# A gated linear unit on one core: the odd tiles' stores issued by GpSimd instead of the scalar engine

## The chip, the cores and the metric

The kernel runs on one core of one Trainium2 chip. The metric is the device time of one execution in microseconds (us); a smaller number is better. The time before is 932.57 us, the median of three runs.

## The reference

```python
x: float32 [8192, 8192]
a, b = np.split(x, 2, axis=-1)
return a * (1 / (1 + np.exp(-b)))      # float32 [8192, 4096]
```

Each output row is the left half of an input row, multiplied element by element by the sigmoid of the right half. So 268 MB are read and 134 MB written.

## The kernel before

A tile is 256 rows of x: 128 partitions with two neighbouring rows each, so that a partition's share of a tile is one contiguous run of 64 KB on the way in and of 32 KB on the way out. There are 32 tiles. Two input buffers `xs` (x_sb in the profile, 64 KB of each partition) and two output buffers `os` (o_sb, 32 KB) are used in turn: tile i uses buffer i % 2 of both, so even tiles have one pair of buffers and odd tiles the other.

`load(i)` (line 63) is a DMA on SyncE's queue, one for a whole tile (two halves for tile 0). `store(i, ...)` (line 68) is a DMA on the scalar engine's queue, one for a whole tile; tile 0 has two pieces of 2 MB, tile 31 one of 2 MB and two of 1 MB. In the profile q1 is SyncE's queue and q10 the scalar engine's.

`work(i, ...)` computes a tile. For tiles 1 to 30 a no-operation on TensorE (line 87) first joins two waits: the tile's load has landed, and the store of tile i-2, which leaves the same output buffer, has landed. Then ScalarE takes the sigmoid of the whole right half in place (line 92). The product (line 97) is split by columns: GpSimd multiplies the first 3/16 (for tile 1 VectorE does), then VectorE the rest; VectorE's instruction waits for GpSimd's. Tiles 0 and 31 are computed in fourths by ScalarE and VectorE alone, so that their stores can start early.

The main loop is: work on tile i, then `load(i + 2)`, then the store of tile i. Both wait for VectorE's product. The order in which each engine gets its instructions is the order of this loop; it is not rearranged (`place` keeps program order and drops the waits that follow from others). On GpSimd's instruction stream there are only the products of tiles 2 to 30, some set-up at the start, and the closing waits and semaphore clears that `_close_on_sync` puts at the end. There SyncE waits for the last store alone; GpSimd waits for the other queues' semaphores and clears them.

Of the kernel before, what the change touches and what calls it, by code (L numbers as in the profile page):

```python
# [8 lines left out]
def _tiles(ctx, tc, x, out):  # L9
    nc = tc.nc  # L10
# [8 lines left out]
    SLOTS = 2  # L19
    n_tiles = n_rows // (P * R)  # L20
    x_g = x.rearrange("(g p h r) m -> g h p (r m)", p=P, h=2, r=R)
    out_g = out.rearrange("(g p h r) m -> g h p (r m)", p=P, h=2, r=R)
# [3 lines left out]
    os = [pool.tile([P, R * half], fp32, name=f"o_sb{k}") for k in range(SLOTS)]  # L26
# [15 lines left out]
    def meet(a, b):  # L42
        return a[0] < b[1] and b[0] < a[1]
# [4 lines left out]
    def place(i, ins, *needs):  # L48


        kept = {n.ins.name for n in needs}
        for e in traced[i % SLOTS]:
            if e.ins.name not in kept:
                tc.declare_no_dep(ins.ins, e.ins, reason="follows from the waits that are kept")
        traced[i % SLOTS].append(ins)
        tc.keep_in_program_order(ins)
        return ins
# [7 lines left out]

    def store(i, lo, hi):
        c = slice(lo * half // 4, hi * half // 4)
        ins = nc.scalar.dma_start(out=out_g[i // 2, i % 2, :, c], in_=os[i % SLOTS][:, c])  # L68
        done = [m for w, m in mul_of[i] if meet(w, (lo, hi))]
        store_of.setdefault(i, []).append(((lo, hi), place(i, ins, *done)))  # L70

# [32 lines left out]
    for i in range(n_tiles):  # L104
        due = list(stores[i])
        for k, piece in enumerate(works[i]):
            work(i, *piece)
            ready = works[i][k - behind[i]][1] if k >= behind[i] else 0
            while len(stores[i]) > 1 and k < len(works[i]) - 1 and due[0][1] <= ready:
                store(i, *due.pop(0))  # L110
        if i + SLOTS < n_tiles:
            load(i + SLOTS)
        for lo, hi in due:
            store(i, lo, hi)
# [115 lines left out]
```

## Time and profile before

| what | value |
|---|---|
| median of 3 runs (lowest to highest) | 932.57 us (932.52 to 932.69) |
| the profiled execution's own time | 932.44 us |
| its span in the profile | 931.1 us |
| busy: VectorE, ScalarE, GpSimd | 232.5, 227.0, 99.3 us |
| moved by DMA | 402.67 MB, mean 432 GB/s |
| issue to landing, median: a whole load, a whole store | 40.0 us, 40.2 us |

The page gives busy times of the compute engines, the share of time in which the core's 16 DMA engines were busy, and the bytes of each DMA queue. The chain of waits names, going back from the last instruction, what released each step. A DMA's "landing" is the time from its issue until its semaphore says that all of it has arrived, so it includes the time spent queued behind other transfers.

### The profile page before, as it was taken

How to read it: one execution, taken by the hardware profiler on the slowest of the kernel's cores; microseconds unless marked ns; L12 is line 12 of the kernel's file. 1: busy time of each engine (PE TensorE's matmuls, PEld its weight loads, DVE VectorE, ACT ScalarE, POOL GpSimd, SP SyncE). 2: the span in 40 equal slices, each digit the busy share in tenths (PEclk: the TensorE clock that was granted, in tenths of full speed). 3: DMA queues.
4: the chain of work that ended last, by engine and by line, in shares of the span. 5: the costliest groups of instructions: out<-in, count | busy, mean ns of one | idle time of the engine just before them, and what ended most of it. 6: DMA issues, size and time to landing. Idle time of an engine off the chain costs nothing.

```text
span 931.1 us, 299 instructions
## 1 busy us (share of the span) xinstructions
DVE 232.5 (25%) x39; ACT 227.0 (24%) x39; POOL 99.3 (11%) x33
## 2 busy tenths in 40 slices
DVE  1133203332023320233302333023330233311333
ACT  2123332033320333202332023320233202333023
POOL 0001110111101111011110111101111011110110
DMA  9999999999999999999999999999999999999998
GB/s 405 450 442 414 428 450 425 453 405 428 450 428 450 410 469 405 428 450 428 450 405 459 420 428 451 425 450 408 431 448 428 450 408 467 408 428 450 427 452 383
DMA packets 9793, 402.67 MB, mean 432 GB/s; under 512 B 1088, under 2 KB 1088, under 8 KB 1088
## 3 DMA queue, kind: packets, MB, share of 16 engines
q1 hardware_dynamic: 4752, 268.44, 66.6%
q10 hardware_dynamic: 5040, 134.22, 33.4%
q14 instruction: 1, 0.01, 0.0%
HBM read 268.44 MB, written 134.22 MB: 432 GB/s over the span
## 4 chain that ended last, share of the span: by engine, by line
DMA 69%; DVE 12%; ACT 12%; POOL 5%; issue 0%; PEldq 0%; ACTq 0%; SPq 0%
DMA out_dram<-o_sb 60%; DVE o_sb L97 12%; ACT x_sb L92 12%; DMA x_sb<-in_x_dram 9%; POOL o_sb L97 5%; PEldq L87 0%; ACTq L68 0%; SPq L63 0%
## 5 line engine op out<-in xcount | busy, mean ns | idle before, releaser
L97 DVE TENSOR_TENSOR o_sb<-x_sb 128x6656 f32<-128x6656 f32 (+2 forms) x39 | 232.5, 5969 | 690.3 <-POOL o_sb L97 632.7
L92 ACT ACTIVATE x_sb<-x_sb 128x8192 f32<-128x8192 f32 (+1 forms) x38 | 225.7, 5949 | 692.7 <-PEq L87 632.9
L97 POOL TENSOR_TENSOR o_sb<-x_sb 128x1536 f32<-128x1536 f32 x29 | 99.1, 3417 | 793.9 <-ACT x_sb L92 793.9
L92 ACT ACT_TABLE_LOAD x1 | 1.3, 1283 | 0.8 <-PEq L214 0.8
L214 POOL MEMSET const-float32-0.0<- 128x1 f32 x1 | 0.1, 99 | 0.2 <-issue 0.2
L214 POOL MEMSET const-bfloat16-1.0<- 128x1 bf16 x1 | 0.1, 103 | 0.0
L214 POOL MEMSET const-uint8-127<- 128x1 uint8 x1 | 0.1, 103 | 0.0
L214 POOL MEMSET const-float32-1.0<- 128x1 f32 x1 | 0.1, 99 | 0.0
## 6 DMA issues: line engine op xcount, KB each, us to landing
out_dram<-o_sb ACTq DMA_DIRECT2D x30, 4096.0 KB, 40.2
x_sb<-in_x_dram SPq DMA_DIRECT2D x2, 4096.0 KB, 16.6
out_dram<-o_sb ACTq DMA_DIRECT2D x3, 2048.0 KB, 27.8
out_dram<-o_sb ACTq DMA_DIRECT2D x2, 1024.0 KB, 8.3
x_sb<-in_x_dram SPq DMA_DIRECT2D x31, 40.0
```

What stands on the lines that cost most here:

```text
L92: before = nc.scalar.activation(out=g, in_=g, func=SIG)
L97: mul = engine.tensor_mul(out=packed[:, r, c], in0=rows[:, r, 0, c], in1=b)
L214: nc = _bacc.Bacc("TRN2", target_bir_lowering=False, num_devices=1)
```

## The change

The store of a tile with an odd number, except the last tile (31), is issued by GpSimd on GpSimd's own DMA queue. The stores of the even tiles and of tile 31 stay on the scalar engine's queue. Those are 15 whole-tile stores, of tiles 1, 3, ..., 29. What is waited for, the buffers, the loads and the arithmetic stay as they are.

```diff
     def store(i, lo, hi):
         c = slice(lo * half // 4, hi * half // 4)
-        ins = nc.scalar.dma_start(out=out_g[i // 2, i % 2, :, c], in_=os[i % SLOTS][:, c])
+        odd = i % 2 and i < n_tiles - 1
+        ins = (nc.gpsimd if odd else nc.scalar).dma_start(out=out_g[i // 2, i % 2, :, c], in_=os[i % SLOTS][:, c])
         done = [m for w, m in mul_of[i] if meet(w, (lo, hi))]
         store_of.setdefault(i, []).append(((lo, hi), place(i, ins, *done)))
```

## The prediction

> **What bounds the kernel now.** I read the page's table of slices and queues first, then one stretch of 58 us in the middle, then the chain of waits, then the end in order of time. The page and the stretch 99.5 to 157.5 (its columns are length, busy VectorE, ScalarE, GpSimd, granted clock, DMA share, GB/s):
>
> ```profile
> DMA  9999999999999999999999999999999999999998
> q1 hardware_dynamic: 4752, 268.44, 66.6%
> q10 hardware_dynamic: 5040, 134.22, 33.4%
> 99.50:157.50 58.00, 14.18 (x2) 14.06 (x2) 6.83 (x2) 1.00 1.00 434
> ```
>
> The DMA engines are busy the whole time, at 434 GB/s. A tile moves 8.39 MB in and 4.19 MB out, 12.58 MB; 12.58 MB / 434 GB/s = 29.0 us, and two tiles make the 58.0 us of the stretch. All 402.67 MB at 434 GB/s are 928 us, so of the 931.1 us of span only some 3 us are not transfer. The change moves no byte less: a gain beyond those 3 us does not exist. The chain of waits for one pair of tiles:
>
> ```profile
> 117.35 40.23 DMA out_dram<-o_sb
> 157.58 0.03 issue
> 157.61 0.06 PEldq L87
> 157.67 0.02 issue
> 157.69 7.04 ACT x_sb L92
> 164.73 0.07 issue
> 164.80 3.43 POOL o_sb L97
> 168.23 0.02 issue
> 168.25 7.10 DVE o_sb L97
> 175.35 0.02 issue
> 175.37 40.19 DMA out_dram<-o_sb
> ```
>
> A buffer's round trip is 40.2 us of store and load in flight and 17.8 us of compute, 58.0 together: exactly two tiles' worth of transfer. The transfers set the 58, and the 40.2 is partly queueing: 29.0 us are service and 40.2 - 29.0 = 11.2 us are spent behind the previous tile's transfer in the same queue. That 11.2 us is the kernel's reserve.
>
> How the two queues share the engines matters here. The counts on the page are 33 loads x 144 packets and 35 stores x 144: 128 of data and 16 small semaphore writes each. A whole load's packet is 64 KB, a whole store's 32 KB; the trace's packet records show 2.418 and 1.213 us for them. Each of the 16 engines has 8 of each per tile. Load and store are issued together and land together (40.0 and 40.2), so the queues alternate one packet each: 8 x (2.418 + 1.213) = 29.0 us.
>
> The end, in order of time (start, length, what):
>
> ```profile
> 871.60 0.36 ACTq L68 DMA_DIRECT2D out_dram<-o_sb  x1
> ...
> 900.61 0.34 ACTq L68 DMA_DIRECT2D out_dram<-o_sb  x1
> 911.66 5.51 ACT L92 ACTIVATE x_sb<-x_sb 128x2048 f32<-128x2048 f32 x3 [21.70 <-DMA x_sb<-in_x_dram]
> ...
> 918.13 0.34 ACTq L68 DMA_DIRECT2D out_dram<-o_sb  x1
> ```
>
> Load 31 lands at 911.3; store 30 (issued 900.61) is what the engines do while tile 31's first half is computed. By the packet records it ends at 920.4 to 921.0 on the sixteen engines. The first piece of store 31 is issued at 918.13, and a DMA on an idle queue moves its first packet 1.0 us after issue (the first load's records), so it is ready at 919.1. The end is covered with 920.4 - 919.1 = 1.3 us to spare.
>
> **Part by part.** (1) ScalarE loses 15 issues of 0.36 us each. They stand in its idle time (22 us before each sigmoid): worth 0.
>
> (2) GpSimd gains 15 issues. Each store waits for VectorE's product of the same tile, as load i+2 does. Queued behind it on GpSimd is its product of tile i+1: store 3 would be issued at 117.35 and that product starts at 136.18 in the timeline, 18.8 us later. What the issue costs GpSimd is not in this trace; the nearest rows are ScalarE's 0.36 us and, as a far end, GpSimd's whole product of 3.42 us. Both vanish in 18.8 us: 0. SyncE's loads have a stream of their own, and TensorE's joining wait only names another semaphore: 0.
>
> (3) The store enters its queue later than from ScalarE, by an amount no row shows. Low end 0; far end one GpSimd instruction, 3.4 us. I take some 1 us, nearer to the 1.0 us of a DMA on an idle queue. It is covered by the 11.2 us that the store no longer spends queued. The Trainium skill (DMA: Bandwidth & Descriptors, Specifications) has about 1 us to the first byte for GpSimd's software-made descriptors and 0.6 us for the others; by these figures the term would be 0.4 us later and still covered. No run here shows it.
>
> (4) The sharing changes. An odd store no longer waits 11.2 us for the even one; for a while three queues take turns, and a turn is 2.418 + 2 x 1.213 = 4.84 instead of 3.63 us, so the load advances more slowly. No work is added: the load lands later by the store packets that overtook it, between one (1.2 us) and the three that fit in the reserve (11.2 / 3.63). Then the store lands earlier (about 30 us after issue, its bare service), the load after some 40 us, and no more packets can overtake. In the middle this costs nothing while the load queue is never empty: a load alone lasts 8 x 2.418 = 19.3 us, and beside a store 29.0, while a landed load needs 17.8 us of compute, and about 1 us to enter, before the next is queued.
>
> (5) The end is where it shows. Store 30 still ends when all transfers before it are done, but load 31 lands one to three packets later, 1.2 to 3.6 us; less the 1.3 us to spare, the engines stand idle for 0 to 2.3 us before store 31. Stepping the turns through the 32 tiles, with two packets taken ahead in each engine (store 0 is issued at 18.57 and first moves at 23.56, 1.0 us of start and about two packets), the load is one or two packets late. I take two: 2.4 - 1.3 = +1.1 us.
>
> (6) GpSimd's closing waits get the new queue's semaphore, done since about 905: 0, up to 0.5 us if its clears fall behind (the closing rows on GpSimd are 17 to 78 ns each and end 1.7 us before the span).
>
> Sum: +1.1 us on the profiled execution, 932.44 + 1.1 = 933.5; the median is 0.13 above that execution, so 933.7. From both ends of (5) and (6) the case spans 0 to +2.8: 932.5 to 935.4. What a measurement can tell from no change is 0.2%, 1.9 us, so to 934.4: this case is mostly "same".
>
> **Rivals.**
>
> *GpSimd's queue takes several packets in a turn.* Then an odd store runs through its 8 packets, 9.7 us, while load and even store stand, and the load that follows runs alone for part of its time. The queue of loads can then run dry: from a load's last byte to the issue of the next are 19.5 us here (881.1 in the packet records to 900.61), and 1 us to enter makes 20.5, against 19.3 us of a load alone. That is up to 1.2 us per pair of tiles, 15 times: 0 to +18 us, in the middle some +6, 939. For it: nothing in this trace forbids it, since GpSimd issues no DMA. Against it: both queues that are seen take one packet a turn. The Trainium skill (DMA: Bandwidth & Descriptors, Queues, rings and completion order) says that an engine drains a whole packet of typically 9 to 17 descriptors before it switches; for the two queues here the rows differ, the turn is a single 64 or 32 KB piece.
>
> *The odd store gets too small a share, or enters too late; this is the slow end.* Place: TensorE's joining wait for tiles 3, 5, ..., 31. It decides as soon as store i lands later than load i+2, about 40 us after issue. Were GpSimd's packets 16 KB, the store would need 16 turns of 2.418 + 0.61, 48.4 us, and 8 packets of the even store fall into them, 9.7: 58 us, 18 later than the load, 15 times: +275, some 1207 us. Were it whole packets but over some 6 us late, stepping the turns gives 5 to 6 us a pair, +80, 1013 us. For it: the reserve is 11 us and each late pair makes the next later. Against: a contiguous run of 32 KB is one packet on the queue seen, and no row of this core's issue is longer than 0.43 us.
>
> *Each packet of the new queue costs a little more on the engines*, 120 per engine: 0.02 to 0.1 us each is +2 to +12 us. The semaphore and data packets of the two queues show no such difference between them.
>
> *Nothing changes at all* (load 31 only one packet late): 932.5, part of my range. *Faster:* a store that starts at once could fill gaps, but all idle time is some 3 us, 1.4 of it the first packet's start and the last semaphore; a gain over 1.9 us has next to no room.
>
> **How the numbers follow.** My case (with "nothing changes" in it) 0.45; several packets a turn 0.22; dearer packets 0.13; too small a share or too late 0.17; faster 0.03. Slower by over 0.2%: 0.07 of my case (two or three packets late), 0.20 and 0.12 of the next two, 0.17: 0.56. Faster 0.03. Same: the rest, 0.41. The likeliest single case gives 933.7, its own range is 932.5 to 935.4; the range must reach over the next two rivals to leave no more than 0.2 out: to 952, the +18 with my term added. Below, 932.0.
>
> **What would show it.** Right: three queues on the page, the new one with 15 x 144 packets and 62.9 MB; DMA share 1.00 in stretches of 58 us; stores landing in about 30 us and loads still in 40; load 31 landing 1 to 4 us later, and a gap of 0 to 2 us before store 31. Several packets a turn: stores of GpSimd landing in 10 to 20 us and loads in the middle preceded by idle engines. Too late or too small a share: GpSimd's stores landing after 45 us or more, ScalarE's sigmoids of odd tiles released by a store, DMA share well under 1. Dearer packets: the stretch of 58 us longer at a share of 1.00. A time under 930.7 would make the whole account wrong.

## The result and the profile after

The changed kernel takes 935.66 us (median of 5 runs, 935.45 to 936.97) against 932.69 us before (5 runs, 932.52 to 932.75): a ratio of 1.0035, 95% interval 1.0024 to 1.0046, some 3 us slower. The profiled execution took 935.52 us, its span is 934.2 us, 3.1 us longer than before.

The middle of the kernel is as fast as before. From the page, the DMA slices, the queues, and the groups of DMA issues (their last column is the median time from issue to landing):

```profile
DMA  9999999999999999999999999999999999999998
q1 hardware_dynamic: 4752, 268.44, 66.4%
q10 hardware_dynamic: 2880, 71.30, 17.7%
q0 software_dynamic: 2160, 62.92, 15.6%
out_dram<-o_sb POOLq DMA_DIRECT2D x15, 4096.0 KB, 34.2
out_dram<-o_sb ACTq DMA_DIRECT2D x15, 4096.0 KB, 32.8
x_sb<-in_x_dram SPq DMA_DIRECT2D x31, 40.3
```

and the same stretch of 58 us as before:

```profile
99.50:157.50 58.00, 14.18 (x2) 14.06 (x2) 7.42 (x3) 1.00 1.00 434
```

There are three queues now; q0 is GpSimd's, with 15 x 144 packets. The stretch still moves 434 GB/s at a share of 1.00. But stores, of both queues, land 33 to 34 us after issue instead of 40.2, and loads still take 40. The chain of waits shows the same turn of roles: one of its round trips is

```profile
142.87 7.10 DVE o_sb L98
149.99 40.21 DMA x_sb<-in_x_dram
190.27 7.04 ACT x_sb L93
```

where before the 40 us were a store. The load has become what lands last. The end in order of time:

```profile
876.65 0.59 POOL L69 DMA_DIRECT2D out_dram<-o_sb  x1 [7.42 <-DVE o_sb L98]
...
904.18 0.34 ACTq L69 DMA_DIRECT2D out_dram<-o_sb  x1
915.46 5.51 ACT L93 ACTIVATE x_sb<-x_sb 128x2048 f32<-128x2048 f32 x3 [21.93 <-DMA x_sb<-in_x_dram]
...
921.93 0.34 ACTq L69 DMA_DIRECT2D out_dram<-o_sb  x1
```

Tile 31's first sigmoid starts at 915.46 instead of 911.66, 3.8 us later, and its first store is issued at 921.93 instead of 918.13, the same 3.8 us. The busy times around 921 us (columns as before: length, VectorE, ScalarE, GpSimd, clock, DMA share, GB/s; a DMA packet is counted here in the stretch in which it starts) show what that does:

```profile
920.50:922.50 2.00, 2.00 (x2) 0.66 (x2) 0.00 (x0) 1.00 0.08 33
```

Between 920.5 and 922.5 packets for only 33 GB/s start. In the kernel before the same two microseconds read

```profile
920.50:922.50 2.00, 2.00 (x1) 0.00 (x0) 0.00 (x0) 1.00 1.03 442
```

So the larger part of the loss is a hole at the end: store 30 is finished and store 31 isn't ready. By the packet records fourteen of the sixteen engines end store 30 at 920.8 to 921.4 and two at 922.1 and 922.3; all of them begin store 31 at 922.8 to 922.9. In the mean of the sixteen the hole is 1.7 us of the 3.1. Another 0.65 us is not a hole: the packets of the whole run took that much longer per engine (931.42 us before, 932.07 now), nearly all of it in loads of the first 100 us.

### The profile page after: what moved, and what is told of

The parts are those of the page before. It is cut to its first block, busy times and chain, and to the rows that moved or that the text cites. A ratio compares the mean times of both kernels' runs of the same rounds, so it can differ in the third digit from the quotient of the medians.

```text
span 934.2 us, 296 instructions
## 1 busy us (share of the span) xinstructions
DVE 232.5 (25%) x39; ACT 227.0 (24%) x39; POOL 108.2 (12%) x48
## 4 chain that ended last, share of the span: by engine, by line
DMA 67%; DVE 12%; ACT 11%; POOL 5%; issue 3%; PEldq 0%; ACTq 0%; POOLq 0%
DMA x_sb<-in_x_dram 63%; DVE o_sb L98 12%; ACT x_sb L93 11%; POOL o_sb L98 5%; DMA out_dram<-o_sb 5%; PEldq L88 0%; ACTq L69 0%; POOLq L69 0%
## 5 line engine op out<-in xcount | busy, mean ns | idle before, releaser
L69 POOL DMA_DIRECT2D out_dram<-o_sb x15 | 9.0, 603 | 166.1 <-DVE o_sb L98 166.1
```

What stands on the lines that cost most here:

```text
L69: ins = (nc.gpsimd if odd else nc.scalar).dma_start(out=out_g[i // 2, i % 2, :, c], in_=os[i % SLOTS][:, c])
```

## The experiments

Two theories stood against each other. *Overtaking:* a store that enters a queue of its own gets ahead of load packets, the loads are late from then on, and the only place that pays is the end. *A price for GpSimd's queue:* each store that GpSimd issues costs something (3 us / 15 = 0.2 us each), or its packets are dearer. The diffs are against the changed kernel, except where the kernel before is named.

**One store instead of fifteen.**

```diff
-        odd = i % 2 and i < n_tiles - 1
+        odd = i == 3
```

> Only the store of tile 3 is issued by GpSimd, the other 14 odd stores go back to the scalar queue. Overtaking theory: one store that enters without queueing moves the loads behind it 3 to 4 us later, and nothing later in the kernel brings them back, because the next stores then find their queue empty; load 31 lands 3 to 4 us later than before and the whole loss of about 3 us is there with one store in fifteen: 935 to 936 us. Rival, a price for each store that GpSimd issues (3 us over 15 stores, 0.2 us each): 932.9 us, and load 31 lands as before.

Measured: 935.99 us, ratio 1.0038 (1.0025 to 1.0050). One store costs as much as fifteen; a price for each is ruled out. The sigmoids of tiles 3 to 7 and then of tile 31, in order of time:

```profile
99.77 7.03 ACT L93 ACTIVATE x_sb<-x_sb 128x8192 f32<-128x8192 f32 x1 [21.98 <-PEq L88]
133.14 7.03 ACT L93 ACTIVATE x_sb<-x_sb 128x8192 f32<-128x8192 f32 x1 [26.34 <-PEq L88]
164.07 7.03 ACT L93 ACTIVATE x_sb<-x_sb 128x8192 f32<-128x8192 f32 x1 [23.90 <-PEq L88]
191.88 7.03 ACT L93 ACTIVATE x_sb<-x_sb 128x8192 f32<-128x8192 f32 x1 [20.78 <-PEq L88]
220.87 7.03 ACT L93 ACTIVATE x_sb<-x_sb 128x8192 f32<-128x8192 f32 x1 [21.96 <-PEq L88]
...
916.84 5.51 ACT L93 ACTIVATE x_sb<-x_sb 128x2048 f32<-128x2048 f32 x3 [21.93 <-DMA x_sb<-in_x_dram]
```

Before, these starts are 99.67, 129.07, 157.69, 186.68, 215.67 and 911.66. The differences are 0.1, 4.1, 6.4, 5.2, 5.2 and, 24 tiles later, 5.2 us. Store 3 enters at about 118 us, the loads behind it are set back, by 6.4 us at most, 1.2 us more than what stays, and remain 5.2 us late (3 to 4 were expected) to the end of the kernel, with nothing on GpSimd's queue any more.

**The same store on a hardware queue.** The kernel before, with store 3 on SyncE's queue ahead of load 5:

```diff
-        ins = nc.scalar.dma_start(out=out_g...
+        ins = (nc.sync if i == 3 else nc.scalar).dma_start(out=out_g...
...
+        if i == 3:
+            store(i, *due.pop())
         if i + SLOTS < n_tiles:
             load(i + SLOTS)
```

> The kernel before, with the store of tile 3 alone put on SyncE's queue, just ahead of load 5; GpSimd issues no DMA. Overtaking theory: a single store that gets ahead of a load shifts the loads for the rest of the kernel, whichever engine issues it; load 31 lands 1 to 5 us later than before and the time rises by 1 to 3.5 us, 933.7 to 936 us. Rival, the loss belongs to GpSimd's software queue: 932.6 us, as before.

Measured: 934.66 us, ratio 1.0022 (1.0013 to 1.0031). Tile 31's sigmoid starts 2.9 us late:

```profile
914.54 5.51 ACT L92 ACTIVATE x_sb<-x_sb 128x2048 f32<-128x2048 f32 x3 [21.85 <-DMA x_sb<-in_x_dram]
```

GpSimd issues no DMA here, and the loads are late all the same: the lateness belongs to the order of packets, not to GpSimd. How it costs time differs. There is no hole at the end of this run, because store 30 ends late as well (921.6 to 922.5 on the sixteen engines, 920.4 to 921.0 before). Its packets took 1.6 us longer per engine, and that is nearly all of the 1.8 us by which the span grew.

**All stores on GpSimd,** first from tile 1:

```diff
+        odd = 0 < i < n_tiles - 1
```

> All stores of tiles 1 to 30 are issued by GpSimd, so that the middle of the kernel has two queues again. Overtaking theory: store i+1 stands behind store i in one queue, as before; only at tile 1 and at the change of queue before tile 31 can a store overtake; 932.5 to 933.7 us, load 31 as before within one store packet (1.2 us). Rival, a price for each store that GpSimd issues: 30 stores, twice the loss, some 939 us.

Measured: 933.90 us, ratio 1.0021 (1.0012 to 1.0030); the runs fall into two groups, 933.5 to 933.9 (6 runs) and 935.1 to 936.6 (5 runs). That is just above the expected range and not the 939 us of a price per store, but load 31 was not within one packet as expected: in the profiled execution, one of the slower group (935.46 us), tile 31's sigmoid starts at 916.36, 4.7 us late. Tile 0's stores were still on the scalar queue, so store 1 overtook tile 0's second piece. The run is confounded by the very effect, and was repeated without the change of queue:

```diff
+        odd = i < n_tiles - 1
```

> All stores of tiles 0 to 30 are issued by GpSimd, so that no store changes its queue until tile 31 and none can overtake in the middle. Overtaking theory: loads land when they did before, within 1 us, and the time is 932.4 to 933.4 us, although GpSimd issues 32 stores. Rival, GpSimd's queue costs something of its own (each store issued some 0.3 us later and 0.6 us of issue, or dearer packets): 934 us or more, with 31 tiles instead of 15 paying.

Measured: 932.87 us, ratio 1.0002 (0.9994 to 1.0011). The groups of issues on its page, and the start of tile 31 in order of time:

```profile
out_dram<-o_sb POOLq DMA_DIRECT2D x30, 4096.0 KB, 40.0
x_sb<-in_x_dram SPq DMA_DIRECT2D x31, 40.1
```

```profile
912.15 5.51 ACT L93 ACTIVATE x_sb<-x_sb 128x2048 f32<-128x2048 f32 x3 [21.74 <-DMA x_sb<-in_x_dram]
```

With 32 stores on GpSimd and one queue for all of them until tile 31, stores land after 40.0 us again and the time is that of before. GpSimd's queue costs this kernel nothing that can be measured.

**Only the last odd store,** tile 29's (`odd = i == 29`):

> Only the store of tile 29, the last odd one before the end, is issued by GpSimd. Overtaking theory: it overtakes what is left of store 28 beside load 30 and load 31, load 31 lands 1 to 5 us later and most of the loss is there: 934 to 936 us. Rival, a price for each store: 932.8 us. A third reading, that the shift has to build up over many tiles: 932.6 to 933 us, with load 31 as before.

Measured: 938.61 us, ratio 1.0064 (1.0051 to 1.0076). More than the expected 936, and nearly twice the loss of the full change. So the shift does not have to build up. With store 3 alone it was largest just after the overtaking (6.4 us at the second sigmoid, 5.2 once settled); that the end comes here before it has settled fits this, and is not shown further. The chain of waits:

```profile
871.93 47.29 DMA x_sb<-in_x_dram
919.22 0.02 issue
919.25 1.92 ACT x_sb L93
```

Load 31 takes 47.3 us instead of 40.0; tile 31 starts 7.6 us late. A load's 144 packets are 128 of data and 16 semaphore writes, one from each engine, and it has landed when the last of these has arrived. Fifteen of load 31's were there by 916.2; the last came 3.1 us later.

Six kernels and the kernel before, one profiled execution each, all in us. "Packets" is how much longer one engine's packets took in all than before, "hole" how much longer the engines were idle between 919 and 929 us (both from the packet records, as the mean of the sixteen engines). "Spread" is the time between the first and the last of load 31's sixteen semaphore arrivals.

| kernel | tile 31 starts | later | span | longer | packets | hole | spread |
|---|---|---|---|---|---|---|---|
| before | 911.66 | | 931.1 | | | | 0.6 |
| all of tiles 0 to 30 on GpSimd | 912.15 | 0.5 | 931.6 | 0.5 | 0.1 | 0.0 | 1.0 |
| store 3 on SyncE | 914.54 | 2.9 | 932.9 | 1.8 | 1.6 | 0.05 | 1.05 |
| the change | 915.46 | 3.8 | 934.2 | 3.1 | 0.65 | 1.7 | 1.5 |
| all of tiles 1 to 30 on GpSimd | 916.36 | 4.7 | 934.1 | 3.0 | 0.7 | 2.55 | 3.7 |
| only store 3 on GpSimd | 916.84 | 5.2 | 934.6 | 3.5 | 2.3 | 1.6 | 2.9 |
| only store 29 on GpSimd | 919.25 | 7.6 | 937.0 | 5.9 | 2.3 | 3.9 | 4.1 |

Except for the first, a span is longer by the lateness of tile 31 less 0.7 to 1.7 us, around the 1.3 us to spare that the prediction read from the trace of before. But the same loss can be made up differently: in the change the hole is the larger part, with store 3 alone the longer packets. What is left of a row lies at the start and after 929 us. And where a store has overtaken, the sixteen engines no longer finish a load together. The first of load 31's arrivals is 2.9 us later than before in the change and also with store 3 alone; the last, for which tile 31 waits, is 3.8 and 5.2 us later.

**Covering the end.** The changed kernel with load 31 in two halves, so that half of tile 31 is there early:

```diff
-    loads[0] = stores[0] = rows
+    loads[0] = stores[0] = loads[-1] = rows
```

> The changed kernel, with load 31 issued as two DMAs of half a tile each, as load 0 is. Overtaking theory with the loss at the end: the first half of tile 31 is there before the whole load would be, its first store piece is ready before store 30 ends, the engines do not fall idle at the end and 1.5 to 3 us come back: 932.5 to 934.2 us. Rival, a loss spread over the middle (a price for each store, slower packets): the end has little to give, 935 us or more.

Measured: 934.01 us (11 runs), ratio 1.0015 (1.0006 to 1.0024): within the expected range. The first piece of store 31 was still issued only at 919.96, behind a sigmoid that waited for the second half. Even so, by the packet records store 31 begins at 920.8 to 921.4, as store 30 ends: the hole is gone with the halves alone. With that order mended as well:

```diff
-            ready = works[i][k - behind[i]][1] if k >= behind[i] else 0
+            late = behind[i] if k > 1 else 0
+            ready = works[i][k - late][1]
```

> The changed kernel with load 31 in two halves, and with the first piece of tile 31's store issued directly after the product it needs (in the run with halves alone it stood in ScalarE's stream behind a sigmoid that waited for the second half, and was issued only at 919.96). Overtaking theory with the loss at the end: first piece ready well before store 30 ends, idle engines at the end gone; what is left is the 0.6 us of longer packets: 932.6 to 933.6 us. Rival, loss in the middle: 934 us or more, as with halves alone.

Measured: 934.22 us, ratio 1.0016 (1.0007 to 1.0025). The first piece is issued at 911.92, and the hole is closed here too, as the busy times show:

```profile
920.50:922.50 2.00, 0.52 (x1) 2.00 (x2) 0.00 (x0) 1.00 0.90 385
```

but the time is 0.6 us above what was expected (the runs range from 933.0 to 936.7), and no better than with halves alone. By the packet records of this execution 15 of the 16 engines write their last semaphore at 930.7 to 931.2, about where the kernel before ends, and one at 933.0. So the hole's share came back on fifteen engines, and one straggler, some 2 us behind, now sets the time of this execution. The lag is not new at the end: already at 104.5 us a load's last semaphore arrives 2.1 us after the fifteenth, and the second half of load 31 is 4.2 us late in the same way (920.0 against 915.8). The run with halves alone has the same straggler (932.9, the other fifteen by 931.1). Why one engine falls behind stays open. The same two changes on the kernel before:

> The kernel before with the same two edits at the end (load 31 in halves, first piece of its store issued directly after its product). Both theories: the kernel before has under half a microsecond of idle engines at its end, so there is next to nothing to gain: 932.0 to 932.8 us.

Measured: 932.72 us, ratio 1.0008 (0.9999 to 1.0018). No gain; no version tried here beats the kernel before.

**The slow rival.** Three runs asked how far the changed kernel is from the collapse that the prediction priced. Odd stores of GpSimd in two DMAs of half the columns, 16 KB packets:

```diff
+        if i % 2 and i < n_tiles - 1:
+            due = rows
         for lo, hi in due:
             store(i, lo, hi)
```

> The changed kernel with each odd store of GpSimd cut into two DMAs of half the columns, so that its packets are 16 KB and it needs 16 turns instead of 8. By the price of the slow rival in the prediction (48.4 + 9.7 = 58 us to landing, 18 us later than the load, 15 times): some 1207 us, GpSimd's second halves landing 55 to 60 us after issue. The other reading, that the engines share by bytes or that halves cost nothing: 934 to 940 us.

Measured: 1232.91 us, ratio 1.322. What ScalarE waited for (total us, times, longest), and then a stretch of 58 us:

```profile
ACT x_sb L93 <- PEq L88: 920.4, 15, 67.9
```

```profile
200.00:258.00 58.00, 14.19 (x2) 13.95 (x2) 7.99 (x4) 1.00 0.64 262
```

The turns are by packets, not by bytes, on GpSimd's queue too: halving the packet halves its share. TensorE's joining wait now holds ScalarE 15 times, once a pair, where in the changed kernel it was 29 times, once for each of tiles 2 to 30 (tile 1 has no earlier store to join). The DMA engines stand idle a third of the time in this stretch. The loss is 20 us a pair; 18 were priced.

Then the odd stores were only made late, by one or two products on a scratch tile ahead of the issue (`n` is 1 or 2):

```diff
+        for _ in range(n if odd else 0):
+            wait = nc.gpsimd.tensor_mul(out=scratch[:, :], in0=scratch[:, :], in1=scratch[:, :])
+            ...   # starts after VectorE's product of the same tile
```

> The changed kernel with one product of 128x2048 on GpSimd, some 4.5 us, between VectorE's product and each odd store's issue; it adds work that the output does not use. GpSimd's stores land 34.2 us after issue and loads after 40.3, so some 6 us are to spare: the store lands just in time and the time stays at 934 to 938 us. Rival, any delay of an odd store costs in full: 15 x 4.5, about 1003 us.

> The same with two such products, some 9.1 us before each odd store. The reserve of about 6 us is used up: stores land after the loads of their tile pair, sigmoids of odd tiles wait for a store, the load queue runs dry; stepping the turns gives 1010 to 1070 us. If the reserve were the whole 11 us that stores used to queue, 934 to 938 us.

Measured: 954.43 us (952.06 and 956.79) and 1027.18 us. A product took 3.6 us, not 4.5. Two of them, 7.2 us, are past the reserve, at the price expected. One alone was expected to be free or to cost in full and does neither. A stretch of each, one product first:

```profile
400.00:458.00 58.00, 14.19 (x2) 14.06 (x2) 10.96 (x4) 1.00 1.01 427
```

```profile
400.00:458.00 58.00, 10.73 (x2) 14.06 (x2) 11.31 (x5) 1.00 0.91 389
```

With two, engines are idle. With one, they are busy the whole time and still move less: what it loses in the middle is lost inside packets. The packet records of loads add up, per engine, to 18.1 us above 2.418 us each, against 1.0 us in the changed kernel and 0.3 before.

## Why the prediction was right or wrong

The time lies in the stated range, 932.0 to 952, at 0.35% slower. In part that is luck. The likeliest case named was +1.1 us, 933.7, with a range of its own that ended at 935.4; the measured 935.66 lies above it, nearly three times as far from the time before. The wider range was there for two rivals that did not happen.

- *What bounds the kernel* held: the middle is 434 GB/s at a share of 1.00, before and after.
- *Parts 1 to 3*, the moved issues, held. GpSimd's issue takes 0.59 us, between the two ends given, and sits in idle time; the store is issued 0.3 us later than the load, and the run with all stores on GpSimd shows that all of it together costs nothing.
- *Part 4*, the overtaking, held in kind, and the run with store 3 alone shows it best. Stores were to land after about 30 us; they took 33 to 34. The text said that no more packets overtake later; that fits the run in which one store is enough. It also said that no work is added, and so put longer packets at nothing: they are 0.65 us of the loss here, and 1.6 and 2.3 us in the runs with store 3 alone.
- *Part 5 is the step that was mis-sized.* Load 31 was taken to be two packets late, 2.4 us; it was 3.8, a little over the three packets (3 x 1.213 = 3.6) of the stated upper end. 3.8 - 1.3 is 2.5 us instead of 1.1 until store 31 can start, and its first packets do start 2.4 us later, at 922.8 instead of 920.4. Of these 2.4 us the engines are idle for 1.7; in the rest they are still busy with store 30, which ends some 0.6 us later; the longer packets account for that. The stepping by turns let one engine stand for all sixteen. The first of load 31's semaphores is 2.9 us later than before, between two and three packets, but tile 31 waits for the last, and these two are 1.5 us apart instead of 0.6. How many packets overtook on each engine was not counted.
- *Part 6*, the end, was put at 0 to 0.5 us for GpSimd's closing waits. These are done at 931.5, ahead of the last store's landing, and cost nothing. What does add some 0.6 us is the last semaphore: in this execution it arrives at 934.16 on one engine, the other fifteen by 933.22. The packet records have one 8 KB packet of the instruction queue q14 there, from 933.00 to 933.31, after the last data packet and before the late semaphore write. It most likely held that write back. The page has two packets of this queue in the run and one for the kernel before. That was not foreseen, and one profiled execution cannot say how often it happens.
- *The rivals.* Several packets in a turn, and dearer packets on the new queue: its 32 KB packets take 1.213 us like the others, and all stores on GpSimd cost nothing. Too small a share or too late did not happen in the change, but its prices stood up: 1207 us were worked out for 16 KB packets, 1232.9 measured, and a delay of 7.2 us past the issue gave 1027 where 1013 had been worked out for "some 6 us late". What had no price is a store that is late by less: 3.6 us cost some 19 us on top of the change. The rule of the Trainium skill that was cited for several packets a turn (DMA: Bandwidth & Descriptors, Queues, rings and completion order: a whole packet of typically 9 to 17 descriptors before an engine switches) does not describe this queue: in the 16 KB run it lost share as a queue does that gets one piece a turn.

## What to carry to other kernels

In a kernel that the DMA engines bound, a second store queue adds no bandwidth; it changes who goes first. A single transfer that gets ahead can shift every later one for the rest of the kernel. That costs longer packets where it happens and a hole at the end, so read the end's cover (here 1.3 us) and don't count on a middle guess: the three packets (3.6 us) that the queueing reserve allows were passed in four kernels of the table, with 3.8 to 7.6 us. A transfer lands with its slowest engine, so one engine does not stand for all sixteen. And where queues take turns by packets, a queue's share is set by its packet size: check that before cutting a transfer in pieces.

## What the hardware showed that was not expected

- One DMA's place in line is kept for the rest of the run: 5.2 us of lateness at 192 us is 5.2 us at 917 us.
- Load packets of 64 KB, which take 2.418 us almost without exception in the kernel before (longest 2.775), grow to as much as 4.2 us around the place where the order changes. In the run with store 3 alone on GpSimd these packets lose 1.5 us per engine between 100 and 200 us, store 3's own another 0.5, and nothing worth naming after that; with every odd store 3.6 us late they lose through the whole kernel, 18 us, with the engines at a share of 1.00. A share of 1.00 is therefore not yet the full rate. What lengthens the packets was not tried. The sixteen engines have fallen out of step where it happens: the semaphore arrivals of one transfer lie 0.2 to 0.7 us apart in the kernel before and up to 12 us apart with every odd store 3.6 us late. Whether this is the cause or goes with it is not shown.
- One 8 KB packet of the instruction queue puts one engine back for the rest of the run. In the kernel before there is one, at 570.0 us, 0.31 us long; the arrivals of a load lie 0.36 us apart at 563.4 and 0.73 us at 592.8. The run with only store 29 on GpSimd has one at 570.3, and there 0.34 us become 0.68.
